# A hybrid decoder layer on one core: four chunks' y kept on chip, x rows apart from B and C, a fourth M buffer, and a sample product over 128 rows

## The chip, the core and the metric

The kernel runs on one core of a Trainium2 chip. The core has five engines with an instruction queue each, worked through in order: TensorE (PE) for products, VectorE (DVE), ScalarE (ACT), GpSimd (POOL) and SyncE (SP), whose queue issues all of this kernel's loads and stores. The metric is the device time of one execution in microseconds (us), as a median over executions. The kernel before takes 1410.79 us (three executions, 1409.48 to 1411.41).

## What is computed

One layer of a decoder, on a prompt of 16 meta rows and 1024 tokens, and on 8 samples of 8 tokens each (1104 rows of 1024 numbers), all in fp32:

```
proj = rmsnorm(h) @ w_in                    # gates b, c, value hv, z, x/B/C, dt
u = c * hv;  ya = group_rmsnorm(b * conv3(u))              # short convolution, 512 wide
xbc = silu(conv4(xbc) + bias);  dt = softplus(dt)          # x 1024 wide, B and C 2 x 128
per chunk of 128 tokens, per head (16 heads of 64):
  y_diag = (C B^T * exp(segment sums of dt*A), lower triangle) @ (dt * x)
  y_off  = C @ S * exp(a_cum);   S = decay * S + B^T @ (decay_end * dt * x)
y = y_diag + y_off + D * x
yb = group_rmsnorm(y * silu(z), 2 groups)
h = h + rmsnorm([ya, yb] @ w_out)
h = h + rmsnorm((silu(fn @ w_gate) * (fn @ w_up)) @ w_down),  fn = rmsnorm(h)
```

A sample has its own state S0 (16 x 64 x 128) and gives back a new one. The outputs are the prompt's and the samples' rows, and the last rows and states of both.

## The kernel before

Products in fp32 are made of two-part splits: an operand is cut into a high part and a low rest, each in a type that TensorE takes at full pace, and a product is three matmuls (high by high, high by low, low by high). Small products (the chunk work) are plain fp32 matmuls.

The program runs in stages. First all x/B/C rows are projected, convolved and written to memory (`d_xbc`). Then one stage mixes two streams: the chunks of the scan with their samples and their ends, and, as a fill between them, the projections that the scan doesn't need: the eight tiles of z (`pz`), then four tiles each of the short convolution's gate c (`pc`, `sconv_gate`), its value (`ph`, `sconv_conv`) and its gate b (`pb`, `sconv_out`). The program hands each piece to a scheduler with a priority, and the scheduler, which goes by its own estimate of when operands are ready, writes the order of every engine's queue when the program is built. The queues of the built program are therefore in another order than the lines of the source; the order is read from the built program.

The parts of this stage that matter here:

- `load_xb(i)` brings chunk i's rows of x, B and C as one tile of 12 blocks, two buffers. `tokens(i)` turns them so that tokens lie on the partitions (`px`, `pb` by transposes) and scales them.
- `y_of(i)` makes the chunk's y. The decay matrix of the 16 heads is built in two tiles M (eight heads each, three buffers): a load of `a_cum` spread over all partitions (`M<-d_a`), eight operations that subtract (DVE L553 for the first tile, ACT L556 for the second), an exponent (ACT L557), a product with the masked C B^T `cb` (DVE L558). Sixteen matmuls (`pd`, L572) give y_diag. y is then written to memory (`d_y`, L579).
- `finish(i)` loads y again with z, multiplies (L588), takes group means by a matmul with ones (`pn`, L596), a root (ACT L597) and a reciprocal (DVE L598), scales (L601), and writes the result (`d_yb`). `FIN` says after which chunk's code each finish stands. `finish(9)`, for the samples, and `finish(8)` stand in the code of the output projection.
- `sample_state(u)`, eight units, gives the new state of four samples and four heads. Its product B^T x (`s1p`) has the split of x in 128 rows: the 64 token rows' high part above the 64 rows' low part (`xs2`). The first matmul (L760) multiplies all 128 rows by B's high part, which stands twice in `b1`; the second (L761) multiplies the upper 64 rows alone by B's low part `b2`, a tile of 64 rows.
- `sconv_out(j)` takes the three column tiles of a `pb` product (256, 320 and 512 columns) out of two accumulators in turn (L662, DVE), squares them (ACT), sums the squares by a matmul (`sn`, L668), takes root and reciprocal (L672) and writes `d_ya`.

The output projection follows (`o`, L1007). Its loop over k begins with the rows that come from the scan: `load_mix` loads `d_yb` of the chunks (`mrb`, L947, two buffers), splits it on ACT (`mhb`, L954) and DVE (`mlb`, L98). Its weights come in as `wo` (three buffers), are scaled and split by ACT (`woh`, L998) and DVE (`wol`, L999). The first group of chunks is 1, 2 and 3. In this passage the last tile of the short convolution (j = 3: `ph3`, `pb3`, with three column tiles 0, 1, 2) and chunk 8 are done beside each other.

Of the kernel before, what the change touches and what calls it, by code (L numbers as in the profile page):

```python
# [16 lines left out]
P = 128  # L17
# [6 lines left out]
LS = 8  # L24
# [10 lines left out]
ROW = 1152  # L35
HPF = 500
NACC = 2
YB = 1
SKIP = NMETA - 4
SAMP = {1: (0,), 2: (1,), 3: (2, 3), 4: (4, 5), 5: (6,), 6: (7,)}  # L40
LATE = (9,)
# [8 lines left out]
ND = 3  # L50
HP4, HP5, HPW = 300, 1000, 300
FILL = [2, 2, 2, 3, 2, 2, 2, 2, 3]
FIN = {4: (1,), 5: (2, 3, 4), 6: (5,), 7: (6,), 8: (7,), 9: (8,)}


@with_exitstack
def hymba_kernel(ctx, tc, x_prompt, x_sample, state_sconv, state_ssm_conv, state_ssm, meta_tokens,
# [5 lines left out]
    V, S, G, PE, SY = nc.vector, nc.scalar, nc.gpsimd, nc.tensor, nc.sync  # L63
# [346 lines left out]
    pf = pfx.__enter__()  # L410
# [4 lines left out]


    def m_tile(name):
        return po.tile([P, 8, P], F32, tag="M", name=name, bufs=3)

    def s_tile(name):  # L420
        return po.tile([P, 8, P], F32, tag="s0", name=name, bufs=2)
# [71 lines left out]

    def load_xb(i):
        t0, w = TT[i]
        xb = po.tile([P, 12, P], F32, tag="xb", name=f"xb{i}", bufs=2)
        for js in (slice(8, 12), slice(0, 8)):
            SY.dma_start(xb[:, js, :w], d_xbc[js, :, t0:t0 + w].rearrange("j p t -> p j t"))
        return xb

    def tokens(xb, i, want_dt):
        t0, w = TT[i]
        px_ = big(f"px{i}")
        for j in range(8):
            PE.transpose(px_[:w, j * P:(j + 1) * P], xb[:, j, :w], ident)
        pb = ps.tile([P, 2 * P], F32, tag="small", name=f"pb{i}", bufs=NSM)
        for g in range(2):
            PE.transpose(pb[:w, g * P:(g + 1) * P], xb[:, 8 + g, :w], ident)
        bt = po.tile([P, 2 * P], F32, tag="btS" if i > NCH else "bt", name=f"bt{i}")
        S.activation(bt[:w], pb[:w], AF.Copy)  # L510
        out = [bt]
        for wgt, nm in ((dt, "xd"), (wdt, "xw")):
            o = po.tile([P, DM], F32, tag=nm, name=f"{nm}{i}")
            src = px_ if nm == "xd" or not want_dt else out[1]
            if nm == "xd" and not want_dt:
                continue
            m = wgt if src is px_ else dend
            V.tensor_tensor(out=o[:w].rearrange("p (h e) -> p h e", h=H),
                              in0=src[:w].rearrange("p (h e) -> p h e", h=H),
                              in1=m[:w, i, :].unsqueeze(2).to_broadcast([w, H, 64]), op=ALU.mult)  # L520
            out.append(o)
        return out

    def y_of(i, xb, bt, xd, off):
# [14 lines left out]
        cb = po.tile([P, 2, P], F32, tag="cb", name=f"cb{i}")  # L539
        mask = U if w == P else Us  # L540
        for g in range(2):
            PE.matmul(pcb[:w, g, :w], xb[:, 8 + g, :w], xb[:, 10 + g, :w], start=True, stop=True)
        V.tensor_tensor(out=cb[:w, :, :w], in0=pcb[:w, :, :w], in1=mask[:w, :w].unsqueeze(1).to_broadcast([w, 2, w]),
                        op=ALU.mult)
        Ms = []
        for g in range(2):
            M = m_tile(f"M{i}{g}")
            SY.dma_start(M[:w, :, :w], d_a[8 * g:8 * g + 8, c, :w].partition_broadcast(w))
            mg = M[:w, :, :w]
            for h in range(8):  # L550
                a_s = a_tok[:w, i, 8 * g + h:8 * g + h + 1]
                if g == 0:
                    V.tensor_scalar(out=M[:w, h, :w], in0=M[:w, h, :w], scalar1=a_s, scalar2=0.0,  # L553
                                    op0=ALU.subtract, op1=ALU.min)
                else:
                    S.activation(M[:w, h, :w], M[:w, h, :w], AF.Relu, scale=-1.0, bias=a_s)  # L556
            S.activation(mg, mg, AF.Exp, scale=1.0 if g == 0 else -1.0)  # L557
            V.tensor_tensor(out=mg, in0=mg, in1=cb[:w, g, :w].unsqueeze(1).to_broadcast([w, 8, w]), op=ALU.mult)  # L558
# [122 lines left out]
    def ssd_chunk(i):  # L681
# [18 lines left out]
    s_nat = state_ssm[0].rearrange("b g e p n -> b (g e p) n")  # L700
    o_nat = o_s_s[0].rearrange("b g e p n -> b (g e p) n")

    def samples_begin():
        i = NCH + 1
        xb = load_xb(i)
# [10 lines left out]
        cv, rv = xb[:, 10:12, :w].rearrange("p g (b i) -> p g b i", i=LS), rest[:, :, :].rearrange("p g (b i) -> p g b i", i=LS)  # L716
# [8 lines left out]
    bms = {}  # L725

    def sample_state(u, st):

# [28 lines left out]
        for q in range(2):  # L757
            xj = slice((j0 + q) * P, (j0 + q + 1) * P)
            o = pt[:, q * 512:(q + 1) * 512]
            PE.matmul(o, xs2[:, xj], b1[:, :, :].rearrange("p b n -> p (b n)"), start=True, stop=False)  # L760
            PE.matmul(o, xs2[0:w, xj], b2[:, :, :].rearrange("p b n -> p (b n)"), start=False, stop=True)  # L761
# [696 lines left out]
```

## Time and profile before

| | |
|---|---|
| median of three executions | 1410.79 us |
| the profiled execution: its own time | 1407.59 us |
| its span, first to last instruction | 1405.9 us |
| TensorE busy | 1371.6 us, 98% |
| VectorE busy | 973.9 us, 69% |
| ScalarE busy | 586.6 us, 42% |
| DMA queue's packets | 53.4% of 16 engines' span |
| mean granted TensorE clock | 0.997 of full speed |

The rows say how long each engine was at work on some instruction. TensorE's matmuls overlap at their ends, so a matmul's own duration (0.39 us for 512 columns) is longer than the distance from one start to the next. Times within a stage are read from the windows of the trace, waits from the view that says for each engine and line which instruction it waited for, and the order of things from the timeline. The stage with the chunks runs from 188 us to about 541 us after the span's start.

### The profile page before, as it was taken

What the parts mean: (1) busy time and instruction counts of PE and PEld (TensorE: products, weight loads), DVE (VectorE), ACT (ScalarE), POOL (GpSimd) and SP (SyncE); (2) the same over time, 40 slices, a digit from 0 to 9 for tenths busy, and PEclk for the clock granted to TensorE, in tenths of its full rate; (3) what the DMA queues carried; (4) which work ended last, traced back from release to release, by engine and by line L of the source; (5) the groups of instructions that cost most, each with busy time, mean ns of one, the idle gap of its engine ahead of it and who ended that gap; (6) DMA issues with size and microseconds to landing.
All of it is one profiled execution on the core that took longest, in us unless ns stands there. A gap on an engine that the chain in (4) does not pass through costs nothing.

```text
span 1405.9 us, 22011 instructions
## 1 busy us (share of the span) xinstructions
PE 1371.6 (98%) x8841; PEld 1229.4 (87%) x8841; DVE 973.9 (69%) x1334; ACT 586.6 (42%) x947; POOL 50.0 (4%) x106
## 2 busy tenths in 40 slices
PE   7999999999999998999999999999999999999997
PEld 5889998878888986887889999999999998888886
DVE  6655457877888987687489877666767666455565
ACT  6465345434354344566554232222332234343431
POOL 1000000000000100011000000000000000000001
PEclk9999999999999999999999999999999999999999
DMA  6135347667736447765445553445333469655554
GB/s 213 47 103 153 94 125 197 204 175 204 216 116 209 130 133 273 249 225 179 149 137 181 183 203 115 161 165 175 133 131 113 163 222 323 226 178 168 168 166 139
DMA packets 212543, 240.51 MB, mean 171 GB/s; under 512 B 33421, under 2 KB 161505, under 8 KB 212442
## 3 DMA queue, kind: packets, MB, share of 16 engines
q1 hardware_dynamic: 212442, 239.12, 53.4%
q8 instruction: 69, 1.13, 0.3%
q14 instruction: 32, 0.26, 0.1%
HBM read 170.29 MB, written 68.79 MB: 170 GB/s over the span
## 4 chain that ended last, share of the span: by engine, by line
PE 84%; DVE 6%; DMA 5%; ACT 2%; issue 1%; SPq 1%; POOL 0%; DVEq 0%; POOLq 0%; ACTq 0%
PE d L1391 15%; PE px L220 10%; PE o L1007 9%; PE yg L1048 7%; PE yu L1048 7%; PE zg L1048 4%; PE zu L1048 4%; PE pz L220 4%; PE xg L1048 4%; PE xu L1048 4%; PE pc L220 3%; PE pb L220 3%; DMA M<-d_a 2%; PE ph L220 2%; PE pd L572 1%
## 5 line engine op out<-in xcount | busy, mean ns | idle before, releaser
L220 PE MATMUL px<-xh,whi 128*128 128x272 f32 (+2 forms) x288 | 94.8, 337 | 0.0
L220 PE MATMUL px<-xl,whi 128*128 128x272 f32 (+2 forms) x288 | 93.7, 333 | 0.0
L220 PE MATMUL px<-xh,wlo 128*128 128x272 f32 (+2 forms) x288 | 93.4, 332 | 0.0
L98 DVE TENSOR_TENSOR wlo<-raw,whi 128x1024 fp32r<-128x1024 f32 x32 | 39.1, 1220 | 44.8 <-ACT whi L106 43.5
L999 DVE SCALAR_TENSOR_TENSOR wol<-wo,vec,woh 128x1024 fp32r<-128x1024 f32 x36 | 46.0, 1278 | 31.5 <-ACT woh L998 31.5
L220 PE MATMUL pz<-xh,whi 128*128 128x256 f32 (+2 forms) x192 | 64.8, 337 | 0.2 <-DVE z L627 0.2
L220 PE MATMUL pz<-xh,wlo 128*128 128x256 f32 (+2 forms) x192 | 63.9, 333 | 0.0
L220 PE MATMUL pz<-xl,whi 128*128 128x256 f32 (+2 forms) x192 | 63.8, 332 | 0.0
L998 ACT ACTIVATE woh<-wo,vec 128x1024 fp32r<-128x1024 f32 x36 | 41.4, 1150 | 49.7 <-PE o L1007 44.1
L220 PEld LDWEIGHTS px<-xh,whi 128*128 128x128 f32 x288 | 54.5, 192 | 4.2
L220 PEld LDWEIGHTS px<-xl,whi 128*128 128x128 f32 x288 | 54.0, 190 | 4.2 <-issue 0.2
L220 PEld LDWEIGHTS px<-xh,wlo 128*128 128x128 f32 x288 | 54.0, 191 | 3.7
L1391 PE MATMUL d<-wd,B01h 128*128 128x512 f32 x176 | 54.2, 389 | 0.0
L252 DVE SCALAR_TENSOR_TENSOR xa<-xr,vec,xa 128x1128 f32<-128x1128 f32 x36 | 50.1, 1391 | 1.2 <-ACT xa L249 0.5
L1391 PE MATMUL d<-wd,T3h 128*128 128x512 f32 x152 | 46.8, 389 | 0.0
L1007 PE MATMUL o<-wol,mhb 128*128 128x512 f32 x144 | 44.3, 393 | 1.4 <-DVE wol L999 1.4
L1391 PE MATMUL d<-wd,B11h 128*128 128x512 f32 x144 | 44.2, 389 | 0.0
L1391 PE MATMUL d<-wd,T2h 128*128 128x512 f32 x144 | 44.2, 389 | 0.0
L556 ACT ACTIVATE M<-M,a_tok 128x128 f32<-128x128 f32 (+1 forms) x72 | 21.7, 383 | 47.8 <-DMA M<-d_a 37.9
L279 ACT ACTIVATE xr<-px 128x272 f32<-128x272 f32 (+2 forms) x36 | 16.3, 456 | 60.0 <-PE px L220 60.0
L1007 PE MATMUL o<-woh,mhb 128*128 128x512 f32 x144 | 39.5, 397 | 1.9 <-DVE gc L662 0.8
L1007 PE MATMUL o<-woh,mlb 128*128 128x512 f32 x128 | 40.0, 390 | 0.0
(691 smaller groups left out, 4094.5 us busy)
## 6 DMA issues: line engine op xcount, KB each, us to landing
wo<-in_w_out_dram SPq DMA_DIRECT2D x36, 512.0 KB, 3.5
raw<-in_w_in_dram SPq DMA_DIRECT2D x32, 512.0 KB, 6.0
wg<-in_w_gate_dram SPq DMA_DIRECT2D x11, 1024.0 KB, 8.4
wu<-in_w_up_dram SPq DMA_DIRECT2D x11, 1024.0 KB, 5.1
xr<-in_w_down_dram SPq DMA_DIRECT2D x11, 1024.0 KB, 5.3
d_t<-xr SPq DMA_DIRECT2D x11, 1024.0 KB
xt<-in_x_prompt_dram SPq DMA_DIRECT2D x16, 512.0 KB, 6.4
M<-d_a SPq DMA_DIRECT2D x16, 512.0 KB, 5.9
```

The costliest lines, as they stand in the source:

```text
L98: V.tensor_tensor(out=out, in0=a, in1=hi.bitcast(F32), op=ALU.subtract)
L220: PE.matmul(acc, (hi, lo, hi)[q][:, wk], (xh, xh, xl)[q][t][:, k, o:], start=n_ == 0, stop=n_ + 1 == len(order))
L252: V.scalar_tensor_tensor(out=dst, in0=part(row, i), scalar=wv[:, wcol(i):wcol(i) + 1], in1=dst, op0=ALU.mult, op1=ALU.add)
L279: S.activation(row[:, rc], pt[:, pc], AF.Copy)
L556: S.activation(M[:w, h, :w], M[:w, h, :w], AF.Relu, scale=-1.0, bias=a_s)
L572: PE.matmul(pdv[64 * e:64 * e + 64, h // 2, :w], xd[:w, h * 64:(h + 1) * 64], Ms[h // 8][:w, h % 8, :w], start=True, stop=True)
L998: S.activation(hi, raw, AF.Copy, scale=nv)
L999: V.scalar_tensor_tensor(out=lo, in0=raw, scalar=nv, in1=hi[:, :].bitcast(F32), op0=ALU.mult, op1=ALU.subtract)
L1007: PE.matmul(accs[i][c], l[:, kb, :], r_[:, c * 512:(c + 1) * 512], start=n == 0 and q == 0, stop=n == 11 and q == len(steps) - 1)
L1048: PE.matmul(acc[:, c, 0:W1], w_[l][k], b[r_][:, k, c * W1:(c + 1) * W1], start=start and k == 0 and x == 0, stop=k == 3 and x == 2, skip_g ...
L1391: PE.matmul(accs[t], sx[x][:, tl], wx[y], start=st and x + y == 0, stop=en and x == 1, skip_group_check=n not in OPENS)
```

## The change

It has five parts.

- The y tiles of chunks 4 to 7 aren't written to memory: `finish` of these chunks works on the tile itself. The tile y has two buffers in place of one; the reloaded yf has one in place of two. `FIN` is changed with it: finish(4) stands after chunk 4, finish(5) and finish(1) after chunk 5, finish(6) and finish(2) after chunk 6, finish(7) and finish(3) after chunk 7. The first three finishes, which still go by memory, so come later, and those of 4 to 7 earlier.
- The tile of 12 blocks becomes two: B and C (`bc`, four blocks, two buffers) and x (`xx`, eight blocks, one buffer).
- M has four buffers in place of three, and both its loads are issued at the head of `y_of`, ahead of those of E.
- The samples' second product runs over 128 rows: `b2` becomes one tile of 128 rows that is held through all units, with its lower 64 rows set to zero once (a copy of a zero block of the identity), so that the product is the same.
- Line numbers move by up to 14 (L947 becomes L961, L662 becomes L672).

```
-YB = 1
+YB = 2
+KEPT = (4, 5, 6, 7)
-FIN = {4: (1,), 5: (2, 3, 4), 6: (5,), 7: (6,), 8: (7,), 9: (8,)}
+FIN = {4: (4,), 5: (5, 1), 6: (6, 2), 7: (7, 3), 9: (8,)}
...
-        return po.tile([P, 8, P], F32, tag="M", name=name, bufs=3)
+        return po.tile([P, 8, P], F32, tag="M", name=name, bufs=4)
...
-        xb = po.tile([P, 12, P], F32, tag="xb", name=f"xb{i}", bufs=2)
-        for js in (slice(8, 12), slice(0, 8)):
-            SY.dma_start(xb[:, js, :w], d_xbc[js, :, t0:t0 + w].rearrange("j p t -> p j t"))
-        return xb
+        bc = po.tile([P, 4, P], F32, tag="bc", name=f"bc{i}", bufs=2)
+        xx = po.tile([P, 8, P], F32, tag="xx", name=f"xx{i}")
+        for dst, js in ((bc, slice(8, 12)), (xx, slice(0, 8))):
+            SY.dma_start(dst[:, :, :w], d_xbc[js, :, t0:t0 + w].rearrange("j p t -> p j t"))
+        return xx, bc
...
+        Ms = [m_tile(f"M{i}{g}") for g in range(2)]
+        for g in range(2):
+            SY.dma_start(Ms[g][:w, :, :w], d_a[8 * g:8 * g + 8, c, :w].partition_broadcast(w))
         for e in range(2):
             SY.dma_start(E[64 * e:64 * e + 64, :, :w],
...
-        SY.dma_start(d_y[i][:, :, :], y)
+        if i in KEPT:
+            kept[i] = y
+        else:
+            SY.dma_start(d_y[i][:, :, :], y)
...
-        y = pf.tile([P, 8, P], F32, tag="yf", name=f"yf{i}", bufs=2)
-        SY.dma_start(y[:, :, :w], d_y[i][:, :, :])
+        if i in KEPT:
+            y = kept.pop(i)
+        else:
+            y = pf.tile([P, 8, P], F32, tag="yf", name=f"yf{i}")
+            SY.dma_start(y[:, :, :w], d_y[i][:, :, :])
...
+        b2 = po.tile([P, 4, P], F32R, tag="bm2", name="bm2")
+        V.tensor_copy(b2[w:2 * w].rearrange("p a (c n) -> p (a c) n", n=w),
+                      ident[w:2 * w, 0:w].unsqueeze(1).to_broadcast([w, 8, w]))
+        bms["lo"] = b2
...
-            PE.matmul(o, xs2[0:w, xj], b2[:, :, :].rearrange("p b n -> p (b n)"), start=False, stop=True)
+            PE.matmul(o, xs2[:, xj], b2[:, :, :].rearrange("p b n -> p (b n)"), start=False, stop=True)
```

How the queues move is read from the built programs. The first place is the DMA queue (SP) at the passage to the output projection. Before, it reads (fso is the prompt's last state, wo_5305 the row block of w_out for k = 7, `d_ya<-gc_4220` the short convolution's tile 2, mrb the first four chunks' rows, post_bc and ffn_bc two norm vectors):

```order
L800 DMA out_dram<-fso 128x8x128
L995 DMA wo_5305<-in_w_out_dram 128x1024
L674 DMA d_ya<-gc_4220 128x1088
L947 DMA mrb_5177<-d_yb_70 128x1024
L947 DMA mrb_5183<-d_yb_71 128x1024
L947 DMA mrb_5189<-d_yb_72 128x1024
L947 DMA mrb_5377<-d_yb_73 128x1024
L859 DMA post_bc<-in_norm_mix_post_dram 128x1024
L861 DMA ffn_bc<-in_norm_ffn_pre_dram 128x1024
L947 DMA mrb_5383<-d_yb_74 128x1024
```

And now (wo_5325 is the row block of k = 8, `d_yb_72<-yf_4518` the end of finish(3), `d_ya<-gc_4217` tile 2 and `d_ya<-gc_4629` tile 3 of the short convolution):

```order
L612 DMA d_yb_72<-yf_4518 128x1024
L594 DMA yf_5285<-d_y_88 128x8x64
L584 DMA d_y_87<-y_4737 128x1024
L684 DMA d_ya<-gc_4217 128x1088
L596 DMA zt_5416<-d_z 128x8x128
L814 DMA out_dram<-fso 128x8x128
L873 DMA post_bc<-in_norm_mix_post_dram 128x1024
L875 DMA ffn_bc<-in_norm_ffn_pre_dram 128x1024
L1009 DMA wo_5325<-in_w_out_dram 128x1024
L961 DMA mrb_5173<-d_yb_70 128x1024
L961 DMA mrb_5179<-d_yb_71 128x1024
```

The loads of mrb stood right behind the store of d_ya's tile 2; now the two norm vectors and the row block of k = 8 stand ahead of them. The block of k = 8 goes to one of three wo buffers, and waits for the split `wol` of k = 5 (DVE) to have read that buffer.

The second place is VectorE's queue ahead of the eviction of `pb3`'s first column tile (`gc<-pb_0`), which frees the accumulator for its third column tile, since there are two. Before (yf_5289 is finish(9), yf_5418 finish(8)):

```order
L649 TENSOR_TENSOR u_4921<-ph_2_4981,gc_4618 128x448
L651 TENSOR_TENSOR u_4921<-ph_2_4981,gc_4618 128x8x8
L999 SCALAR_TENSOR_TENSOR wol_5202<-wo_5199,vec,woh_5201 128x1024
L673 TENSOR_TENSOR gc_4220<-gc_4220,sq_4849 128x512
L252 SCALAR_TENSOR_TENSOR gc_4618<-u_4921,vec,gc_4618 128x1024
L252 SCALAR_TENSOR_TENSOR gc_4618<-u_4921,vec,gc_4618 128x64
L588 TENSOR_TENSOR yf_5418<-yf_5418,zt_5420 128x1024
L252 SCALAR_TENSOR_TENSOR gc_4618<-u_4921,vec,gc_4618 128x1024
L252 SCALAR_TENSOR_TENSOR gc_4618<-u_4921,vec,gc_4618 128x64
L593 TENSOR_TENSOR zt_5420<-zt_5420 128x2x256
L662 TENSOR_TENSOR gc_4618<-pb_0_5022,gc_4618 128x256
```

Now there is finish(3)'s reciprocal (`sg_4524`) and scaling (`yf_4518`), chunk 8's cb and M, and the three reciprocals of the short convolution's tile 2 (`sq_4845`), in two pieces that follow each other without a gap:

```order
L608 RECIPROCAL sg_4524<-sg_4524 128x256
L659 TENSOR_TENSOR u_4917<-ph_2_4977,gc_4629 128x448
L661 TENSOR_TENSOR u_4917<-ph_2_4977,gc_4629 128x8x8
L1013 SCALAR_TENSOR_TENSOR wol_5198<-wo_5195,vec,woh_5197 128x1024
L611 TENSOR_TENSOR yf_4518<-yf_4518,sg_4524 128x512 x2
L548 TENSOR_TENSOR cb_4745<-pcb_4744,U 128x256
L253 SCALAR_TENSOR_TENSOR gc_4629<-u_4917,vec,gc_4629 128x1024
L253 SCALAR_TENSOR_TENSOR gc_4629<-u_4917,vec,gc_4629 128x64
L682 RECIPROCAL sq_4845<-sq_4845 128x256
```

```order
L561 TENSOR_TENSOR M_4738<-M_4738,cb_4745 128x1024
L561 TENSOR_TENSOR M_4739<-M_4739,cb_4745 128x1024
L253 SCALAR_TENSOR_TENSOR gc_4629<-u_4917,vec,gc_4629 128x1024
L253 SCALAR_TENSOR_TENSOR gc_4629<-u_4917,vec,gc_4629 128x64
L682 RECIPROCAL sq_4845<-sq_4845 128x320
L683 TENSOR_TENSOR gc_4217<-gc_4217,sq_4845 128x256
L682 RECIPROCAL sq_4845<-sq_4845 128x512
L598 TENSOR_TENSOR yf_5285<-yf_5285,zt_5287 128x8x64
L672 TENSOR_TENSOR gc_4629<-pb_0_5018,gc_4629 128x256
```

Chunk 8's M products and the reciprocals of tile 2 stood ahead of `u<-ph_2` before, and stand behind it now, between it and the eviction.

The third place is VectorE's queue a little later, up to the splits of `wol` and `mlb`. Before, the `wol` of k = 4 is in the piece above, and there follow:

```order
L662 TENSOR_TENSOR gc_4618<-pb_1_5056,gc_4618 128x320
L98 TENSOR_TENSOR mlb_5180<-mrb_5177,mhb_5179 128x1024
L98 TENSOR_TENSOR mlb_5186<-mrb_5183,mhb_5185 128x1024
L98 TENSOR_TENSOR mlb_5192<-mrb_5189,mhb_5191 128x1024
L672 RECIPROCAL sq_5048<-sq_5048 128x128 x2
L672 RECIPROCAL sq_5048<-sq_5048 128x160 x2
L662 TENSOR_TENSOR gc_4618<-pb_2_5089,gc_4618 128x512
L98 TENSOR_TENSOR mlb_5380<-mrb_5377,mhb_5379 128x1024
L999 SCALAR_TENSOR_TENSOR wol_5226<-wo_5223,vec,woh_5225 128x1024
```

Now the reciprocals of tile 3, the last eviction and the `wol` of k = 5 come ahead of the first `mlb`:

```order
L682 RECIPROCAL sq_5044<-sq_5044 128x128 x2
L682 RECIPROCAL sq_5044<-sq_5044 128x160 x2
L672 TENSOR_TENSOR gc_4629<-pb_2_5085,gc_4629 128x512
L683 TENSOR_TENSOR gc_4629<-gc_4629,sq_5044 128x256
L1013 SCALAR_TENSOR_TENSOR wol_5222<-wo_5219,vec,woh_5221 128x1024
L683 TENSOR_TENSOR gc_4629<-gc_4629,sq_5044 128x320
L682 RECIPROCAL sq_5044<-sq_5044 128x256 x2
L848 COPY slo<-slp 18x512
L608 RECIPROCAL sg_5291<-sg_5291 128x2x64
L683 TENSOR_TENSOR gc_4629<-gc_4629,sq_5044 128x512
L611 TENSOR_TENSOR yf_5285<-yf_5285,sg_5291 128x4x64 x2
L99 TENSOR_TENSOR mlb_5176<-mrb_5173,mhb_5175 128x1024
```

The three `mlb` moved from ahead of the reciprocals to behind them and behind `wol` of k = 5.

More of the change, by code (lines that the diff above doesn't have):

```diff
@@ L504, in tokens @@
         for j in range(8):
-            PE.transpose(px_[:w, j * P:(j + 1) * P], xb[:, j, :w], ident)
+            PE.transpose(px_[:w, j * P:(j + 1) * P], xb[0][:, j, :w], ident)
         pb = ps.tile([P, 2 * P], F32, tag="small", name=f"pb{i}", bufs=NSM)
         for g in range(2):
-            PE.transpose(pb[:w, g * P:(g + 1) * P], xb[:, 8 + g, :w], ident)
+            PE.transpose(pb[:w, g * P:(g + 1) * P], xb[1][:, g, :w], ident)
         bt = po.tile([P, 2 * P], F32, tag="btS" if i > NCH else "bt", name=f"bt{i}")
@@ L541, in y_of @@
         for g in range(2):
-            PE.matmul(pcb[:w, g, :w], xb[:, 8 + g, :w], xb[:, 10 + g, :w], start=True, stop=True)
+            PE.matmul(pcb[:w, g, :w], xb[1][:, g, :w], xb[1][:, 2 + g, :w], start=True, stop=True)
         V.tensor_tensor(out=cb[:w, :, :w], in0=pcb[:w, :, :w], in1=mask[:w, :w].unsqueeze(1).to_broadcast([w, 2, w]),
                         op=ALU.mult)
-        Ms = []
         for g in range(2):
-            M = m_tile(f"M{i}{g}")
-            SY.dma_start(M[:w, :, :w], d_a[8 * g:8 * g + 8, c, :w].partition_broadcast(w))
+            M = Ms[g]
             mg = M[:w, :, :w]
@@ L558, in y_of @@
             V.tensor_tensor(out=mg, in0=mg, in1=cb[:w, g, :w].unsqueeze(1).to_broadcast([w, 8, w]), op=ALU.mult)
-            Ms.append(M)
         if not smp:
@@ L564, in y_of @@
         for j in range(8):
-            S.activation(y[:, j, :w], xb[:, j, :w], AF.Copy, scale=Dp[:, j:j + 1])
+            S.activation(y[:, j, :w], xb[0][:, j, :w], AF.Copy, scale=Dp[:, j:j + 1])
         if not smp:
@@ L578, in y_of @@
             return E, y
-        SY.dma_start(d_y[i][:, :, :], y)
+        if i in KEPT:
+            kept[i] = y
+        else:
+            SY.dma_start(d_y[i][:, :, :], y)
+    kept = {}
     def finish(i):
         t0, w = TT[i]
-        y = pf.tile([P, 8, P], F32, tag="yf", name=f"yf{i}", bufs=2)
-        SY.dma_start(y[:, :, :w], d_y[i][:, :, :])
+        if i in KEPT:
[3 more added lines that the diff above has]
+            SY.dma_start(y[:, :, :w], d_y[i][:, :, :])
         zt = pf.tile([P, 8, P], F32, tag="zt", name=f"zt{i}")
@@ L689, in off @@
             for j in range(8):
-                PE.matmul(pov[:, j, :], cur[:, j * P:(j + 1) * P], xb[:, 10 + j // 4, :], start=True, stop=True)
+                PE.matmul(pov[:, j, :], cur[:, j * P:(j + 1) * P], xb[1][:, 2 + j // 4, :], start=True, stop=True)
         y_of(i, xb, bt, xd, off)
@@ L701, in hymba_kernel @@
     o_nat = o_s_s[0].rearrange("b g e p n -> b (g e p) n")
+    bms = {}
     def samples_begin():
@@ L713, in samples_begin @@
         V.tensor_tensor(out=bt[w:2 * w], in0=bt[:w], in1=bh[:w].bitcast(F32), op=ALU.subtract)
+        b2 = po.tile([P, 4, P], F32R, tag="bm2", name="bm2")
+        V.tensor_copy(b2[w:2 * w].rearrange("p a (c n) -> p (a c) n", n=w),
+                      ident[w:2 * w, 0:w].unsqueeze(1).to_broadcast([w, 8, w]))
+        bms["lo"] = b2
         cs = po.tile([P, 2, NS, 3, LS], BF16, tag="cS", name="cS")
         rest = po.tile([P, 2, P], F32, tag="cb", name="cR")[:, :, :w]
-        cv, rv = xb[:, 10:12, :w].rearrange("p g (b i) -> p g b i", i=LS), rest[:, :, :].rearrange("p g (b i) -> p g b i", i=LS)
+        cv, rv = xb[1][:, 2:4, :w].rearrange("p g (b i) -> p g b i", i=LS), rest[:, :, :].rearrange("p g (b i) -> p g b i", i=LS)
         for g in range(2):
@@ L723, in samples_begin @@
         return xs2, bt, cs, E, y
-    bms = {}
     def sample_state(u, st):
@@ L736, in sample_state @@
             b1 = po.tile([P, 4, P], F32R, tag="bm1", name=f"bm1{u}")
-            b2 = po.tile([w, 4, P], F32R, tag="bm2", name=f"bm2{u}")
+            b2 = bms["lo"]
             mk = [bd8[h:h + w, tl].rearrange("p (b i) -> p b i", i=LS)[:, :, 0:1].to_broadcast([w, 4, P]) for h in (0, w)]
-            for dst, h in ((b1[0:w], 0), (b1[w:2 * w], 0), (b2, w)):
+            for dst, h in ((b1[0:w], 0), (b1[w:2 * w], 0), (b2[0:w], w)):
                 V.tensor_tensor(out=dst, in0=bt[h:h + w, g * P:(g + 1) * P].unsqueeze(1).to_broadcast([w, 4, P]),
```

## The prediction

> **What bounds the kernel now.** I read the page's span, then the windows of the stage that is changed.
>
> ```profile
> span 1405.9 us, 22011 instructions
> ```
>
> The columns of the windows are length, busy time of PE, weight loads, DVE, ACT and POOL, the granted clock, the DMA share and GB/s.
>
> ```profile
> 188.00:550.00 362.00, 351.51 (x2396) 299.67 (x2394) 292.00 (x396) 159.38 (x302) 11.29 (x14) 1.00 0.62 180
> 500.00:530.00 30.00, 29.53 (x196) 25.45 (x194) 27.88 (x32) 13.99 (x21) 1.32 (x2) 1.00 0.42 131
> 530.00:550.00 20.00, 15.20 (x57) 11.33 (x58) 13.62 (x17) 9.84 (x13) 0.00 (x0) 0.91 0.79 282
> ```
>
> TensorE is the bound: it stands idle for 362.0 − 351.5 = 10.5 us of the stage. So a change pays where it takes matmul time away, or one of these idle microseconds, and costs where TensorE starts to wait. Nearly half of the idle time, 4.8 us, lies in the 20 us of the passage to the output projection. Just ahead of it VectorE is busy for 27.9 of 30 us: there, what is put in VectorE's way is soon paid by TensorE. The timeline of TensorE shows the wait, and what a wait does to the matmuls behind it (start, duration, and in brackets the idle time before):
>
> ```profile
> 533.14 0.80 PE L220 MATMUL pb<-xh,whi 128*128 128x512 f32 x1 [3.61 <-DVE gc L662]
> 533.73 0.63 PE L220 MATMUL pb<-xh,wlo 128*128 128x512 f32 x1
> 534.16 0.63 PE L220 MATMUL pb<-xl,whi 128*128 128x512 f32 x1
> ...
> 536.93 0.39 PE L220 MATMUL pb<-xh,wlo 128*128 128x512 f32 x1
> 537.16 0.39 PE L220 MATMUL pb<-xl,whi 128*128 128x512 f32 x1
> ```
>
> The third column tile of pb3 waits until VectorE has emptied an accumulator (3.61 us). After it the matmuls start 0.43 us apart (533.73 to 534.16), later 0.23 (536.93 to 537.16): (536.93 − 533.14 − 0.25) / 0.43 is about seven slow ones and some at full pace, 7 × 0.2 = 1.4 us more, with the window's clock at 0.91. I call this the cold start, since it follows an idle time.
>
> **The sample product.** One unit's four products, and what the same shape costs where all have 128 rows (the chain's row of the output projection):
>
> ```profile
> 312.28 0.40 PE L760 MATMUL s1p<-bm,xs 128*128 128x512 f32 x1
> 312.61 0.50 PE L761 MATMUL s1p<-bm,xs 64*128 64x512 f32 x1
> ...
> 313.90 0.71 PE L773 MATMUL so<-cS,s0t 128*128 128x8 bf16 x22
> ...
> 566.03 44.62 PE o L1007 x196
> ```
>
> The four take 313.90 − 312.28 = 1.62 us. Of 128 rows each a matmul takes 44.62 / 196 = 0.228 us, so four are 0.91. The saving is 0.71 × 8 units = **5.7 us** of TensorE time, on the path. What the row shows is a slow pace wherever 64 rows meet 128, not that the row count makes it; if it isn't the row count, the saving is zero (a rival below). The added copy of zeros is one VectorE operation of 512 columns over 64 rows, once, early; the window from 188 leaves VectorE 70 us idle, so it costs nothing there, and under 0.7 us without that cover.
>
> The Trainium skill, "TensorE: Matmul & The Clock Gate", in the section "Why this matters for your kernels", says that a single matmul over few rows takes the same time as one over 128 rows, and so speaks against this edit; by it the term is 0 and the sum 5.7 us higher. This trace has 0.43 us a piece where 64 rows alternate with 128, against 0.228; that the row count is the cause it doesn't show.
>
> **Kept y, x rows with one buffer, M.** The kept y takes away four stores and four loads of 512 KB. They run on the DMA queue at a share of 0.62 and TensorE never waits for them, so this gives nothing by itself. The one x buffer means that the next chunk's x can't be loaded until the transposes and the D·x copies of this chunk are done; the stage has 362 us for eight chunks, 45 each, and the longest landing in this text is 6.7, so I take 0; where chunk 0, the samples and chunk 1 follow each other closely, up to 2 us can be lost. For M the waits of the stage (total, times, longest) matter:
>
> ```profile
> DVE M L553 <- DMA M<-d_a: 15.2, 7, 4.0
> PE s0p L750 <- DVE s L766: 2.2, 1, 2.2
> ```
>
> VectorE stands before M's load seven times, and in one of them a sample unit's eviction is caught behind it and TensorE loses 2.2 us. The order of the changed program puts the loads of chunk i + 2 right behind chunk i's products, with VectorE's operations on them close behind, so VectorE still waits, in other places. I take 1 us gained; from 5.3 (all that TensorE loses in the stage outside the waits of the passage, 10.5 − 3.6 − 0.8 − 0.8) to −4 (two more catches of the size of the one shown) are possible.
>
> **The passage.** This is the large term. VectorE's queue now has finish(3), chunk 8's M and the reciprocals of the short convolution's tile 2 between ph3's last tile and the eviction that pb3's third tile waits for. The prices (last number ahead of the bar: busy total; behind the comma: mean ns):
>
> ```profile
> L598 DVE RECIPROCAL sg<-sg 128x256 f32<-128x256 f32 x7 | 12.2, 1745 | 0.7 <-ACT sg L597 0.7
> L999 DVE SCALAR_TENSOR_TENSOR wol<-wo,vec,woh 128x1024 fp32r<-128x1024 f32 x2 | 2.6, 1278 | 0.0
> L601 DVE TENSOR_TENSOR yf<-yf,sg 128x512 f32<-128x512 f32 x14 | 8.9, 677 | 0.0
> L252 DVE SCALAR_TENSOR_TENSOR gc<-u,vec,gc 128x1024 f32<-128x1024 f32 x8 | 10.0, 1253 | 0.9 <-ACT gc L249 0.9
> L672 DVE RECIPROCAL sq<-sq 128x256 f32<-128x256 f32 x3 | 5.1, 1707 | 0.0
> L672 DVE RECIPROCAL sq<-sq 128x320 f32<-128x320 f32 x3 | 6.4, 2144 | 0.0
> L672 DVE RECIPROCAL sq<-sq 128x512 f32<-128x512 f32 x3 | 10.0, 3325 | 0.0
> L558 DVE TENSOR_TENSOR M<-M,cb 128x1024 f32<-128x1024 f32 x16 | 19.0, 1217 | 1.3 <-ACT M L557 1.2
> ```
>
> Let F be the moment when TensorE has done 20 of the 24 matmuls of ph3's third tile; behind them its queue has finish(3)'s pn, on which VectorE's reciprocal waits. In us: 1.75 + 1.28 + 2 × 0.68 + 2 × 1.25 + 1.71 + 2.14 + 3.33 + 2 × 1.22 = 16.5, and ten small pieces (u, cb, the 64-column taps, evictions), by estimate 0.3 each, 3; less about 0.06 of overlap per instruction, 1.2; ahead of it pn and its root, 1. So the accumulator is free at about F + 19.3. TensorE's own work until then, from the chain of waits:
>
> ```profile
> 504.25 1.02 PE pd L572 x16
> 506.31 1.72 PE st L608 x4
> 511.80 0.43 PE pn L596 x2
> 515.68 0.54 PE sn L668 x2
> 516.68 0.86 PE sn L668 x2
> 517.54 4.78 PE ph L220 x21
> 522.76 2.81 PE pb L220 x24
> ```
>
> pn 0.43, four left of ph3 0.91 (21 take 4.78), pb3's first tile 2.81, its second 24 × 0.228 × 320/512 = 3.4, the three sn of tile 2 0.43 + 0.54 + 0.86, two halves of chunk 8's pd 2.04, its st 1.72, small transposes and cb 0.7: 13.9. It waits 5.4 us, and 1.4 for the cold start, against 3.6 + 1.4 before: **+1.8**. TensorE is then through 20 matmuls of pb3's third tile at E.
>
> What follows is new. Before, the mrb loads were issued while TensorE still had this tile to do, and its first `o` came 0.2 us behind the last pb. The rows are TensorE's timeline, and below them the chain of waits:
>
> ```profile
> 540.90 0.39 PE L220 MATMUL pb<-xl,whi 128*128 128x512 f32 x1
> 541.12 0.63 PE L1007 MATMUL o<-woh,mhb 128*128 128x512 f32 x2
> ...
> 545.53 1.42 PE L1007 MATMUL o<-woh,mhb 128*128 128x512 f32 x5 [0.82 <-ACT woh L998]
> 547.79 0.50 PE L1007 MATMUL o<-woh,mhb 128*128 128x512 f32 x1 [0.84 <-DVE gc L662]
> ```
>
> ```profile
> 530.04 6.71 DMA mrb<-d_yb
> 536.76 1.07 ACT mhb L954
> ...
> 539.11 4.25 DMA mrb<-d_yb
> ...
> 543.41 3.78 DVE sq L672 x4
> 547.19 0.56 DVE gc L662
> ```
>
> Now the first mrb load stands behind the row block of k = 8, which waits for `wol` of k = 5, which stands in VectorE's queue behind the four reciprocals of tile 3 and the last eviction. From E: sn and root 1.0, reciprocals 3.8, eviction 0.6, small scaling 0.3, wol 1.3: E + 7.0; issue of two DMAs 0.5; landing between 4.25 and 6.71, I take 5.5; mhb 1.1; the first `o` at E + 14. TensorE's own work until then is two sn 1.0, four matmuls 0.9, the state's transposes 0.9 (as `px` of eight), sn 0.9, small ones 0.9: 4.6. So it waits 9.5 us, and starts cold: 1.5. The third chunk's mrb waits for a buffer, that is for mlb of chunk 1, and lands about a microsecond late; `wol` of k = 6 is late by about 1.5, and takes the place of the two waits of 0.82 and 0.84 in the rows above. Sum of this part: 9.5 + 1.5 + 1.0 = **+12**.
>
> **The sum**: −5.7 − 1 + 1.8 + 12 = **+7** us. The profiled execution (1407.59, of it 1405.9 span) lies 3.2 us under the median 1410.79; added to the median, 1417.8. A measurement of this kernel can tell about 0.2%, 2.8 us, from no change.
>
> The same page of the Trainium skill, section "HAM oscillation", says that an idle time longer than about 3.4 us halves TensorE's clock. The trace's 3.61 us of idle with matmuls at 0.43 us behind it agrees; the sum has the cold start by the rows alone.
>
> **The rivals.**
> *Faster.* The M loads give more than I grant. Place: the chunks, where the loads come one chunk ahead. For it: VectorE's 15.2 us before M. Price: the passage costs 13.8, the sample product gives 5.7, so M must give 8.1 to break even and 10.9 to be seen; TensorE's idle time outside the passage is 5.3. It must therefore also loosen VectorE's lag in the passage, by the landing at its quicker end (1.3) and by a queue 5 us shorter. Then 1410.8 − 5.7 − 5.3 + 13.8 − 6.3 = 1407. Against it: in the passage VectorE waits for pn, which lies on TensorE's queue, so a lead of VectorE doesn't come through. 0.13.
> *No change.* The mrb chain is as said, but VectorE reaches the eviction as before and M gives 4: −5.7 − 4 + 10 = 0, 1411. 0.13.
> *Slower by more, in the chunks.* The single x buffer and the M operations catch TensorE twice more, +4 in place of −1: 1423. 0.14.
> *The sample product gives nothing.* The weights of one row count and the next are loaded slowly for another cause (the split operand, the change of type to and from bf16): 1423.5. This is the page's rule. For it: the first of the four is slow too, though it has 128 rows; against it: 196 matmuls with weights of the same size at 0.228. 0.07.
> *The forecast*, +3 to +11: 0.53.
>
> **How the numbers follow.** Slower by over 0.2%: 0.53 + 0.14 + 0.07 = 0.74; within: 0.13; faster: 0.13. The forecast's own range, from landing (±1.3), VectorE's small pieces (±1.5) and M (±2): 1413.5 to 1422. With the other cases, leaving out one in ten at either end: 1408 to 1425.
>
> **What would show it.** Right: sixteen s1p matmuls of L775 with 128 rows 0.23 us apart; a wait of TensorE for gc's eviction (L672) of about 5.4 us, then one of 6 or more for mhb; mrb's first load issued after pb3's last matmul; a second window with a clock under 1. Wrong: `o` right behind pb3 as before, or L775 at 0.43 us; or more than 5 us of new waits of TensorE in the chunks.

## The result and the profile after

The changed kernel takes 1423.76 us (median of six executions, 1422.52 to 1429.64), against 1411.10 for the kernel before, run beside it (six executions). The ratio is 1.0094, with a 95% interval of 1.0071 to 1.0116: 10 to 16 us slower. The forecast was 7 us, with a range of its own up to 1422 us; the median lies 1.8 us above that, inside the wider range to 1425. The profiled execution takes 1422.54 us, its span is 1420.8.

TensorE's waits over the whole span (engine and line, what it waited for, then total, times and longest in us):

```profile
PE o L1021 <- ACT mhb L968: 7.0, 1, 7.0
PE pz L221 <- DVE z L637: 5.1, 3, 3.1
PE pb L221 <- DVE gc L672: 5.0, 1, 5.0
PE sn L678 <- ACT sq L676: 3.3, 1, 3.3
...
PE o L1021 <- DVE wol L1013: 2.5, 2, 1.4
```

Three of these are the passage to the output projection as forecast: the accumulator's eviction (5.0), and between pb3 and the first `o` 3.3 + 7.0. The windows, with the last one of the kernel before beside them (length, busy PE, weight loads, DVE, ACT, POOL, clock, DMA):

```profile
188.00:550.00 362.00, 342.73 (x2377) 298.43 (x2376) 289.77 (x393) 148.08 (x286) 6.17 (x14) 0.98 0.55 156
500.00:530.00 30.00, 26.82 (x176) 22.57 (x175) 24.72 (x29) 7.51 (x11) 1.32 (x2) 1.00 0.28 88
530.00:560.00 30.00, 17.17 (x57) 12.88 (x58) 21.15 (x27) 8.16 (x12) 0.00 (x0) 0.73 0.71 242
```

```profile
530.00:560.00 30.00, 25.20 (x103) 19.57 (x104) 23.62 (x28) 13.07 (x16) 0.00 (x0) 0.94 0.75 270
```

From 530 to 560 us TensorE is busy for 17 of 30 us at a granted clock of 0.73; before (second piece) it was 25 us at 0.94. TensorE's timeline in that stretch (start, duration, idle time before):

```profile
532.25 0.79 PE L221 MATMUL pb<-xh,whi 128*128 128x512 f32 x1 [4.96 <-DVE gc L672]
...
536.25 0.58 PE L221 MATMUL pb<-xh,whi 128*128 128x512 f32 x1
...
545.14 1.13 PE L678 MATMUL sn<-sq,bd 128*128 128x512 f32 x2 [3.26 <-ACT sq L676]
...
554.52 1.22 PE L1021 MATMUL o<-woh,mhb 128*128 128x512 f32 x2 [6.99 <-ACT mhb L968]
555.55 1.05 PE L1021 MATMUL o<-wol,mhb 128*128 128x512 f32 x2
...
559.81 0.96 PE L1021 MATMUL o<-wol,mhb 128*128 128x512 f32 x2
...
561.53 0.62 PE L1021 MATMUL o<-woh,mhb 128*128 128x512 f32 x2
```

pb3's third tile begins at 532.25, 0.9 us earlier than before (533.14). The first `o` begins at 554.52, 13.4 us later than before (541.12). So 14.3 us are lost between these two, 22.3 us in place of 8.0; what stands behind the first `o` adds 1.5, and the spans differ by 14.9. Ahead of the third tile the change has gained only 0.9. The forecast's chain is there on VectorE and on the DMA queue:

```profile
513.97 1.75 DVE L608 RECIPROCAL sg<-sg 128x256 f32<-128x256 f32 x1 [5.01 <-ACT sg L607]
...
531.79 0.80 DVE L672 TENSOR_TENSOR gc<-pb,gc 128x256 f32<-128x256 f32 x2
...
540.10 3.79 DVE L682 RECIPROCAL sq<-sq 128x128 f32<-128x128 f32 x4 [3.58 <-ACT sq L679]
...
544.67 1.28 DVE L1013 SCALAR_TENSOR_TENSOR wol<-wo,vec,woh 128x1024 fp32r<-128x1024 f32 x1
```

```profile
543.14 0.38 SPq L814 DMA_DIRECT2D out_dram<-fso  x1
543.61 0.53 SPq L873 DMA_DIRECT2D post_bc<-in_norm_mix_post_dram  x1
544.20 1.12 SPq L875 DMA_DIRECT2D ffn_bc<-in_norm_ffn_pre_dram  x1
545.98 0.33 SPq L1009 DMA_DIRECT2D wo<-in_w_out_dram  x1
546.35 1.11 SPq L961 DMA_DIRECT2D mrb<-d_yb  x2
```

VectorE stands 5 us, waiting for the root that follows finish(3)'s pn, then works 18 us without a gap until it frees the accumulator. The two mrb loads go out at 546.35, just behind the row block of k = 8, which had waited for that `wol` (544.67 + 1.28). But the store of the prompt's last state, four places ahead, had itself gone out only at 543.14. Before, the loads were issued at 529.54. From the issue at 546.35 to the first mhb, which waited for the load, 7.1 us pass (553.41); the forecast had 5.5.

In the chunks there is a wait that the forecast didn't have: TensorE's longest stop before a z tile, and what ScalarE did ahead of that tile:

```profile
268.50 0.64 PE L221 MATMUL pz<-xh,whi 128*128 128x320 f32 x1 [3.13 <-DVE z L637]
...
273.74 0.35 PE L221 MATMUL pz<-xh,wlo 128*128 128x320 f32 x1
```

```profile
263.85 1.58 ACT L559 ACTIVATE M<-M,a_tok 128x128 f32<-128x128 f32 x5 [8.43 <-DMA M<-d_a]
265.33 1.04 ACT L560 ACTIVATE M<-M 128x1024 f32<-128x1024 f32 x1
266.28 0.97 ACT L559 ACTIVATE M<-M,a_tok 128x128 f32<-128x128 f32 x3
267.15 0.58 ACT L636 ACTIVATE z<-pz 128x512 f32<-128x512 f32 x1
```

ScalarE stood 8.4 us before M's load; the z tile that TensorE waited to have emptied stood behind it in the queue. Behind this wait the matmuls start 0.27 us apart until 273.74, in place of 0.147 (the rows from 274.08 on): some 2.4 us more, with the granted clock at 0.81 from 262 to 280 us (1.00 before). ScalarE also stands, over the stage, before x and before the store of a kept y:

```profile
ACT y L567 <- DMA xx<-d_xbc: 20.4, 5, 7.7
ACT y L567 <- DMA d_yb<-y: 13.9, 2, 9.2
```

And the sample product, of four matmuls:

```profile
303.13 0.48 PE L774 MATMUL s1p<-bm,xs 128*128 128x512 f32 x1
303.44 0.40 PE L775 MATMUL s1p<-bm,xs 128*128 128x512 f32 x1
303.67 0.39 PE L774 MATMUL s1p<-bm,xs 128*128 128x512 f32 x1
303.90 0.39 PE L775 MATMUL s1p<-bm,xs 128*128 128x512 f32 x1
304.13 0.71 PE L787 MATMUL so<-cS,s0t 128*128 128x8 bf16 x22
```

They take 304.13 − 303.13 = 1.00 us in place of 1.62, so 5.0 us less over eight units.

### The profile page after: what moved, and what is told of

Its sections match the earlier page's. It is cut to its first block, busy times and chain, and to the rows that moved or that the text cites. A ratio compares the mean times of both kernels' runs of the same rounds, so it can differ in the third digit from the quotient of the medians.

```text
span 1420.8 us, 22005 instructions
## 1 busy us (share of the span) xinstructions
PE 1371.7 (97%) x8841; PEld 1234.0 (87%) x8841; DVE 975.5 (69%) x1335; ACT 581.4 (41%) x943; POOL 44.9 (3%) x106
## 4 chain that ended last, share of the span: by engine, by line
PE 84%; DVE 8%; DMA 4%; ACT 2%; issue 1%; SPq 0%; POOL 0%; DVEq 0%; POOLq 0%; ACTq 0%
PE d L1405 14%; PE px L221 10%; PE o L1021 9%; PE yg L1062 7%; PE yu L1062 7%; PE pz L221 5%; PE zg L1062 4%; PE zu L1062 4%; PE xg L1062 4%; PE xu L1062 4%; PE pc L221 3%; PE pb L221 3%; DMA M<-d_a 2%; PE ph L221 2%; DVE sq L682 1%
## 5 line engine op out<-in xcount | busy, mean ns | idle before, releaser
L221 PEld LDWEIGHTS pz<-xh,whi 128*128 128x128 f32 x192 | 37.1, 193 | 9.2 <-DVE z L637 6.1
L221 PEld LDWEIGHTS pz<-xl,whi 128*128 128x128 f32 x192 | 37.0, 193 | 3.8 <-issue 1.2
```

What stands on the lines that cost most here:

```text
L221: PE.matmul(acc, (hi, lo, hi)[q][:, wk], (xh, xh, xl)[q][t][:, k, o:], start=n_ == 0, stop=n_ + 1 == len(order))
```

## The experiments

The theory after the result: the passage costs some 15 us through the place of the finishes in the queues; the sample product gives 5 to 6; the chunks lose some 4 through M's early loads or the single x buffer. The rivals differ from run to run. All runs are compared with the kernel before on the same chip; "TensorE's waits" is the sum of its rows in the waits view from 188 to 600 us of the profiled execution (kernel before: 10.2, changed kernel: 24.5). The changed kernel wasn't run again beside these runs; where one is set against it, medians of different rounds are compared, and its interval (1.0071 to 1.0116) has to be kept in mind.

**The 128 rows alone.**

```
-            b2 = po.tile([w, 4, P], F32R, tag="bm2", name=f"bm2{u}")
+            b2 = bms["lo"]
...
-            PE.matmul(o, xs2[0:w, xj], b2[:, :, :].rearrange("p b n -> p (b n)"), start=False, stop=True)
+            PE.matmul(o, xs2[:, xj], b2[:, :, :].rearrange("p b n -> p (b n)"), start=False, stop=True)
```

> The kernel before with the samples' second product over 128 rows and nothing else. My theory (the row count of the weights sets the pace): 8 units x 0.71 us = 5.7 us less, about 0.4%, with both products 0.23 us apart. Rival (the slow pace has another cause, the change of type between neighbours): 0.43 us a piece stays, and the time stays within 1 us of the kernel before.

1409.58 against 1410.63 us, ratio 0.9994 (0.9979 to 1.0009): no difference that can be told. The matmuls did become quick (0.39 us median duration in both lines, in place of 0.49 and 0.50), but TensorE's waits rose from 10.2 to 14.9:

```profile
PE s0p L754 <- DVE s L770: 3.7, 1, 3.7
...
PE so L777 <- ACT s0t L756: 2.5, 2, 1.4
```

```profile
298.31 0.28 DVE L553 TENSOR_SCALAR M<-M,a_tok 128x128 f32<-128x128 f32 x1 [4.71 <-DMA M<-d_a]
```

TensorE came to the next unit's transposes 0.4 us earlier and waited there for VectorE, which waited for M's load longer, 4.71 us in place of 3.97. Of some 5 us, 4.7 came back as waits (1.5 of them here), and the matmuls behind the 3.7 us start 0.27 us apart, in place of 0.147, from 304.65 to 307.73: 1.4 us more. Theory and rival were each half right: the pace was the row count's, the time stayed.

**The change without the 128 rows.** The same edit the other way, in the changed kernel.

> The changed kernel with the samples' second product over 64 rows again, all other parts of the change kept. My theory: 5.7 to 6.2 us slower than the changed kernel, so 18 to 20 us (1.3%) slower than the kernel before. Rival (VectorE, not TensorE, is what the sample units wait for once TensorE is quicker): the same as the changed kernel, 12 to 13 us slower than before.

1426.91 us, ratio to before 1.0119 (1.0095 to 1.0143). The changed kernel's is 1.0094: the edit is worth some 3 us there, between the two expectations, and the intervals overlap.

**The 128 rows with VectorE relieved.** Two kernels, in which the samples' state decay is left out:

```
-        for q in range(2):
-            V.tensor_tensor(out=s0[:, 4 * q:4 * q + 4, :], in0=s0[:, 4 * q:4 * q + 4, :],
-                            in1=Ev[:, q, :, LS - 1:LS].to_broadcast([P, 4, P]), op=ALU.mult)
```

> The kernel before without the samples' state decay (two VectorE operations of 0.65 us in each of the eight units are left out, so the new sample states lack their decay), product over 64 rows. Only the base for the next kernel. VectorE loses 10 us of work in the chunks: if VectorE were the bound there, 3 us or more faster than before; if TensorE is, the same.

> The kernel before without the samples' state decay, as no_decay_64, and with the product over 128 rows. Theory 3 (the 5.7 us of TensorE time are eaten by waits for VectorE, whose queue is as long as before): with VectorE relieved the 128 rows bring 4 to 6 us against no_decay_64. Rival (they are eaten by waits for loads and by the order of the queues, whatever VectorE's load): 0 to 2 us against no_decay_64.

With 64 rows 1408.31 us, 0.9990 (0.9979 to 1.0001): VectorE's 10 us by themselves are worth nothing that can be told. With 128 rows 1406.22, 0.9973 (0.9961 to 0.9985): 2.1 us between the two, at the edge of the rival's 0 to 2 and well under the theory's 4 to 6. The profiled executions differ by more, 1406.5 against 1401.9 us of span, with waits of 9.9 and 10.9; but that is one execution each. The theory isn't borne out, and that relief lets more through than the 1.0 us of rows128_only isn't shown.

**The kept y and the finishes alone** (with the 128 rows; x and M as before).

```
-YB = 1
+YB = 2
+KEPT = (4, 5, 6, 7)
...
-FIN = {4: (1,), 5: (2, 3, 4), 6: (5,), 7: (6,), 8: (7,), 9: (8,)}
+FIN = {4: (4,), 5: (5, 1), 6: (6, 2), 7: (7, 3), 9: (8,)}
...
```

> The kernel before with the 128 rows, the kept y and the new order of the finishes; x, B and C in one tile with two buffers and M with three buffers, loaded as before. My theory (the passage to the output projection pays for the order of the finishes): the wait for the eviction, 5 us, and that for mhb, 10 us, are there; about +16 - 6 = 10 us (0.7%) slower than the kernel before. Rival (the x and M part costs): 5 to 6 us faster than before.

1429.42 us, ratio 1.0138 (1.0108 to 1.0168): 19 us slower, more than the whole change. TensorE's waits are 31.0. Of these 4.5 are for u and 3.5 for a sample state, in the chunks; the passage is as forecast:

```profile
PE o L1020 <- ACT mhb L967: 9.1, 2, 8.2
...
PE pb L221 <- DVE gc L671: 4.2, 1, 4.2
...
PE sn L677 <- ACT sq L675: 3.0, 1, 3.0
```

ScalarE shows why the kept y isn't free. Its row in this kernel:

```profile
ACT y L566 <- DMA d_yb<-y: 21.3, 3, 9.2
```

The next y can't be begun until the finish two chunks back has been stored. What stands behind in ScalarE's queue waits with it.

**x and M alone** (with the 128 rows; y and the finishes as before).

> The kernel before with the 128 rows, the split x and B, C tiles and the four M buffers with their loads first; y goes by memory and the finishes stand as before. My theory (M's early loads put ScalarE's wait ahead of a z eviction, +4 us, and the passage stays as before): -6 + 4, so 2 us faster than before, not told from no change. Rival (M's loads or the single x buffer make the passage long): 8 us or more slower. Other rival (they gain): 9 us or more faster.

1423.98 us, ratio 1.0096 (1.0068 to 1.0123): 13 us slower; the theory fell, the rival holds in size but not in place: the waits (27.2) are in the chunks (7.2 for z, 4.1 for u, 2.9 for z again), and in the passage mainly the eviction's 3.5 (3.6 before).

**x alone, and M's loads alone** (both with the 128 rows; M's loads first with three buffers, since a fourth has no room beside two x buffers).

```
-        xb = po.tile([P, 12, P], F32, tag="xb", name=f"xb{i}", bufs=2)
...
+        bc = po.tile([P, 4, P], F32, tag="bc", name=f"bc{i}", bufs=2)
+        xx = po.tile([P, 8, P], F32, tag="xx", name=f"xx{i}")
```

> The kernel before with the 128 rows and the split of x from B, C, x with one buffer; M, y and the finishes as before. Theory 1 (the single x buffer is what the chunks pay for: ScalarE's D.x copies stand before the late load, and the evictions of the fill stand behind them): 8 to 13 us slower than before, with new waits of ScalarE before xx. Theory 2 (M's early loads are what the chunks pay for): within 2 us of the kernel before.

> The kernel before with the 128 rows and M's two loads issued together at the head of y_of, with three M buffers; x, y and the finishes as before. Theory 1 (the single x buffer is the cost): within 2 us of the kernel before. Theory 2 (M's early loads put ScalarE's and VectorE's waits ahead of evictions): 5 to 13 us slower, with TensorE waiting for z and u.

x alone: 1419.37 us, 1.0061 (1.0038 to 1.0084), 9 us slower, waits 22.0. M's loads: 1409.00 us, 0.9985 (0.9967 to 1.0004), waits 12.0. So it is the single x buffer, not M's loads, that the chunks pay for in this setting. The place is not the expected one: ScalarE waits before xx for only 2.1 us in x_only (20.4 in the changed kernel). TensorE's waits are spread over many places, the longest 4.1, 3.4 and 2.7 us, and the order of all queues differs.

**The finishes back in order**, in the changed kernel.

```
-FIN = {4: (4,), 5: (5, 1), 6: (6, 2), 7: (7, 3), 9: (8,)}
+FIN = {4: (1, 4), 5: (2, 5), 6: (3, 6), 7: (7,), 9: (8,)}
```

> The changed kernel, all parts kept, with finish(1), (2), (3) standing ahead of finish(4), (5), (6): FIN = {4: (1, 4), 5: (2, 5), 6: (3, 6), 7: (7,), 9: (8,)}. In its queues finish(3) and the reciprocals of tile 2 are gone from the passage and the first three mrb loads stand ahead of the norm vectors and of the row block of k = 8. My theory (the passage pays 16.8 us through finish(3)'s place): 12 to 16 us faster than the changed kernel, so -3 to +1 us against the kernel before. Rival (the passage is long because chunk 8 is late, whatever stands in it): at most 4 us faster than the changed kernel, 9 to 12 us slower than before.

1414.57 us, 1.0033 (1.0018 to 1.0049): 9 us faster than the changed kernel, less than the theory's 12 to 16 and far more than the rival's 4. Up to the first `o` the passage is whole again, on TensorE's timeline and on the DMA queue:

```profile
541.20 0.63 PE L1021 MATMUL o<-woh,mhb 128*128 128x512 f32 x2
...
545.60 0.73 PE L1021 MATMUL o<-woh,mhb 128*128 128x512 f32 x2 [0.59 <-ACT mhb L968]
...
556.46 1.22 PE L1021 MATMUL o<-wol,mhb 128*128 128x512 f32 x2 [2.34 <-DVE wol L1013]
```

```profile
532.47 0.62 SPq L814 DMA_DIRECT2D out_dram<-fso  x1
533.14 8.16 SPq L961 DMA_DIRECT2D mrb<-d_yb  x3
```

The wait for the eviction of pb3's first tile is gone from TensorE's waits, the mrb loads go out at 533.14, and of 10.3 us before `o` 0.6 are left, while the later wait for `wol` has grown from 1.0 to 2.3. The first `o` begins at 541.20, as early as in the kernel before (541.12), although TensorE waits in the chunks 5.8 us for z and 4.5 for c's eviction, the latter a wait that the changed kernel hasn't. So the 4.5 us by which the spans of the two profiled executions differ (1410.4 and 1405.9) come behind the first `o`: among them the 2.3 us and the slow matmuls after it, which run until 559.9. ScalarE's wait for d_yb falls from 13.9 to 4.2 us.

**Only the mrb loads moved**, by a higher priority.

```
-    load_mix("b", GROUPS[0])
+    with tc.high_priority(offset=HPW):
+        load_mix("b", GROUPS[0])
```

> The changed kernel with the first mrb loads given a higher priority: in the DMA queue two of them move ahead of the row block of k = 8 and of the two norm vectors, right behind the store of the prompt's last state; the rest is as in the changed kernel. By my prediction's step (mrb waits for the wol of k = 5 through the row block of k = 8) they are issued up to 3 us earlier in this trace, 543.5 in place of 546.4, since the state's store went out at 543.1: 3 us faster than the changed kernel, 10 us slower than before. Rival (that place in the queue is the whole wait of 10 us): 9 to 10 us faster than the changed kernel.

1421.48 us, 1.0084 (1.0058 to 1.0110), 2.3 us faster than the changed kernel. The intervals overlap, so the gain itself isn't clear of the noise, but it fits the step's 3 us, and the rival's 9 to 10 us are ruled out. The store of the last state goes out at 541.89 here, the two loads at 542.33, and a third only at 550.84:

```profile
542.33 1.75 SPq L961 DMA_DIRECT2D mrb<-d_yb  x2
...
550.84 0.35 SPq L961 DMA_DIRECT2D mrb<-d_yb  x1
```

```profile
PE o L1022 <- ACT mhb L968: 6.1, 2, 4.0
```

The wait for the first mhb shrinks (2.0 in place of 7.0), and the third chunk's gives another 4.0; the waits for the eviction (5.0) and for sn (3.3) are those of the changed kernel. So the row block of k = 8 was the last of several things late at once; that the rest of the lateness comes from finish(3) and chunk 8 is read from the queues and isn't separated by a run.

**Two x buffers**, with three for M, with the finishes of the change and with the finishes in order.

> The changed kernel with two buffers for x and three for M (the same memory), all else kept. Theory 1 (in the changed kernel too, the single x buffer is what the chunks pay for; the passage stays as it is): 4 to 10 us faster than the changed kernel, 3 to 9 us slower than before. Theory 2 (with y kept, the copies of y wait for the buffer of y and its store, and the x buffer is no longer the last to come): within 2 us of the changed kernel, 11 to 13 us slower than before.

> The same with finish(1), (2), (3) ahead of finish(4), (5), (6): what is left of the change are the kept y, M's early loads and the 128 rows. By theory 1 and the run of early_finish: 1414.6 - 4 to 10 us, so 6 us faster to the same as before, the first of these kernels that may beat it. By theory 2: 1412 to 1415, 2 to 4 us slower than before.

With the finishes of the change: 1427.27 us, 1.0120 (1.0100 to 1.0141), 3.5 us more than the changed kernel, with overlapping intervals: theory 1's gain of 4 to 10 us isn't there. TensorE's waits (27.6) are in the passage and in the chunks as in the changed kernel. ScalarE's wait for xx falls from 20.4 to 3.6 us, but its wait for M, of which there are three buffers here, rises from 13.2 to 45.0. With the finishes in order: 1404.16 us, 0.9956 (0.9939 to 0.9973), as theory 1 has it: the one version of the change that beats the kernel before, by 4 to 9 us. All waits of TensorE over a microsecond in this stretch, 188 to 600 us:

```profile
PE pz L221 <- DVE z L637: 3.1, 1, 3.1
PE sn L678 <- ACT sq L676: 2.7, 1, 2.7
PE o L1021 <- DVE wol L1013: 2.2, 1, 2.2
PE so L787 <- ACT s0t L766: 1.6, 1, 1.6
```

TensorE's waits are 10.7, about those of the kernel before, with the sample product's saving on top. ScalarE's wait for d_yb, 15.6 us in two_x, is 6.1.

## Why the prediction was right in direction and short in size

*The passage* (+1.8 and +12, 13.8 in all) was right, step by step: the eviction's wait 5.0 for 5.4 forecast; VectorE's stretch from finish(3)'s reciprocal to the eviction 513.97 to 532.2, 18 us, for 18.3; the `wol` of k = 5 done 7.0 us after E (538.95 to 545.95), as forecast; the first `o` 15.6 us after E, for 14, since the mrb load took 7.1 and not 5.5. early_finish, which alters only the places of the finishes, makes the first `o` wait vanish. The cold start was under-sized: 1.4 and 1.5 us were forecast; the ten starts from 532.25 to 536.66 take 2.1 us more than at 0.228 us each, the fourteen from 554.52 to 560.61 2.9. The Trainium skill, "TensorE: Matmul & The Clock Gate", section "What's actually happening", says that the full clock comes back after at least one busy window of about 3.4 us; the slow stretches here, 3.1 to 6.1 us long, lie on both sides of that, and the trace decides.

*What holds the loads* was only half right. The forecast named the row block of k = 8; mrb_ahead shows that this place is worth some 2 us of the timed 12.7, not clear of the noise, and that the store of the last state, and so chunk 8, is late as well.

*The sample product* (−5.7, "5.7 us of TensorE time, on the path") failed in its second half. As TensorE time it is 5.0; as time of the kernel it is 1.0 alone (rows128_only, within the noise) and some 3 in the changed kernel (rows64_again, intervals overlapping). TensorE is busy for 97% of the stage, but the saving turned into waits for loads and evictions, 4.7 us of them in rows128_only. That the queues of VectorE and ScalarE pace the chunks is read from these waits; the two kernels without the decay didn't settle it. The rival on this point, that the pace had another cause than the row count, is refuted: with 128 rows the same operands start 0.23 us apart. The Trainium skill, "TensorE: Matmul & The Clock Gate", section "Why this matters for your kernels", speaks of a single matmul, which with few rows takes as long as with 128; where 64 and 128 rows alternate, these runs have 0.43 us a piece against 0.23.

*The chunks* (−1 for M, 0 for x) were wrong in sign, and this is the largest miss. TensorE's waits in them are 7.9 us against 5.0 before, the 5.1 for z among them, and the slow stretch behind the longest wait is 2.4 more: +5.3 in place of −1. That ScalarE stood before M's load ahead of it is shown for the longest of these waits. The prediction put x at nothing because 45 us a chunk seemed enough for a landing of 6.7; ScalarE stood 20.4 us before xx, and x_only, with one x buffer, is 9 us slower, while M_first loses nothing. The costs of the parts (0, 9 and, for kept_y, 19) don't add up to the change's 13. The rival "slower by more, in the chunks" had the right kind of wait, and its sum, 1423, is what was measured; the prediction's sign for it, more than 5 us of new waits in the chunks, is met by the z and u waits (5.1 and 1.6), while the old ones for s0p and c are nearly gone.

The terms in the profiled pair, as an estimate from these rows: −5.0 from the sample product, +5.3 in the chunks, and +14.9 in the passage (waits of 16.6 against 5.2, and 2.1 + 2.9 − 1.5 = 3.5 of slower matmuls). Their sum is 15.2; the spans differ by 14.9, where 7 was forecast. So the sample product paid for the chunks (some of whose waits are its own saving come back: rows64_again has waits of 22.8 in place of 24.5), and the passage, nearly as large as forecast, is left as the whole loss. Against the forecast the passage is 1.1 off, the sample product 0.7 and the chunks 6.3, all in one direction: the place of the loss was foreseen, and not that nothing would pay for it.

What stays open: through which queue the single x buffer costs x_only its 9 us, and why two x buffers bring nothing with the late finishes but 10 us with the early ones. The early finishes do free the kept y earlier (ScalarE's wait for d_yb 4.2 in place of 13.9); how much of their 9 us that is, and how much the order of VectorE's queue, wasn't separated. Nor was the reloaded yf, which has one buffer in place of two wherever y is kept. With three M buffers two_x_early_finish wins; four beside two x buffers have no room.

## What to carry to other kernels

Where an engine is busy for 97% of a stage, price a saving on it by a run of that edit alone: the waits before and after tell what arrives (here 5.0 us of matmul time, waits from 10.2 to 14.9, time −1.0, within the noise). When a step is put later, read off the built queues what now stands between it and the next stage's first loads; here the late finishes cost 9 us, and their place was to be seen in VectorE's and the DMA queue's order before any run. A tile kept on chip to save a load is freed by the store of its last reader, and whoever writes the next tile waits for that in order, with all that stands behind.

## What the runs showed of the hardware

In the sample product, matmuls whose weights have 64 rows, alternating with ones of 128 rows, start 0.43 us apart at 512 columns; with 128 rows throughout 0.23 us. The rows of the weight loader (PEld) show the difference, first the kernel before, then the changed one:

```profile
313.04 0.19 PEld L760 LDWEIGHTS s1p<-bm,xs 128*128 128x128 f32 x1 [0.25 <-issue]
```

```profile
303.44 0.19 PEld L774 LDWEIGHTS s1p<-bm,xs 128*128 128x128 f32 x1
```

With alternating rows the weight load begins when its own matmul does (313.04), after 0.25 us in which the loader stood still; with 128 rows it begins 0.23 us ahead of its matmul (303.67), beside the one before.

The stretch of slow matmuls behind an idle time of TensorE had no fixed length and didn't follow the last idle time alone: none behind 2.2 us (kernel before, at 302.57), 3.4 us behind 2.3 (early_finish, at 556.46), 5.2 behind 3.1 (changed kernel, at 268.50), 3.1 behind 3.6 (kernel before, at 533.14), and in the changed kernel's passage 4.4 behind 5.0 and 6.1 behind 7.0.
